# One prefill-and-stream step of a hybrid layer on one core: PSUM banks, linear-attention exponentials, output norm and the up-to-down seam rearranged

## The chip, the cores and the metric

The kernel runs on one core of a Trainium2 chip. A core has TensorE (PE, matrix products into the PSUM banks), VectorE (DVE), ScalarE (ACT), GpSimd (POOL) and SyncE (SP, which mostly issues transfers). The metric is the device time of one execution in microseconds (us): 1954.07, the median of three runs (1953.86 to 1955.78).

## The reference, cut to what matters

```python
h = rms_norm(x, g_pre_mix)
qa, ka, va, ra, alr, qb, kb, vb, ga, gb = split_cols(h @ w_in)
oa, s_gla = gla_branch(qa, ka, va, ra, alr, w_a2, b_a2, g_gla, gla_s0, gla_block)
ob, k_rows, v_rows = attn_fn(qb, kb, vb, rel_bias)
mix = (jax.nn.sigmoid(ga) * (oa @ w_br_a) + jax.nn.sigmoid(gb) * (ob @ w_br_b)) @ w_out
x = x + rms_norm(mix, g_post_mix)
f, conv_new = conv_ffn(rms_norm(x, g_pre_ffn), conv_s0, w_up, conv_w, conv_b, w_down)
x = x + rms_norm(f, g_post_ffn)
gate = jax.nn.sigmoid(rms_norm(x, g_pre_ple) @ w_ple_gate)
x = x + rms_norm(gate * (pe @ w_ple), g_post_ple)
...
# gla_branch, per head, b = cumulative log decay inside a block
decay = exp(where(j <= i, b[i] - b[j], -inf)); scores = sum_c q[i,c] k[j,c] decay[i,j,c]
o = scores @ v + (q * exp(b)) @ S;  S = exp(b_last) * S + (k * exp(b_last - b)).T @ v
o = rms_norm_per_head(o) * g_gla * silu(r)
```

There are 1024 prompt tokens and 32 sample tokens with the same weights, 1056 columns in all, D_MODEL 1024, four linear-attention heads (key 128, value 256), eight band-attention heads and a feed-forward width of 2816. All is fp32.

## The kernel before, in words

Activations lie with features on the 128 partitions and the 1056 tokens along the free dimension. An fp32 product is three matmuls on split operands: high times high, low times high, high times low (L230 to L232, L804 to L806, L1911 to L1913, L2356 to L2358). A split costs an ACT copy of the high half and a DVE subtraction for the low half. The wide layers (in, up, down) use one level of Strassen, so their products land in pairs of banks.

The eight PSUM banks are divided by `repsum` into three rotating sets: `mm` for the dense products, `one` for small ones, `two` for pairs. A matmul that wants the next bank of a set waits until that bank's last reader is done. In the band and linear-attention stages the division is `PS_BAND`: 3 `mm`, 3 `one`, 1 pair.

The stages that the change touches come in this order:

- *In-projection* (`in_strassen`, to 300 us): makes q, k, v and the gates; the gate rows silu(r) go to DRAM.
- *Band attention* (300 to 596 us) and *linear attention* (596 to 930 us). In both, units of a dense product (24 matmuls into one `mm` bank, L804 to L806, evacuated by ACT at L710 or L728 or by DVE at L786) fill the gaps of a chain of small steps; `piece()` issues a third of a unit, `flush()` evacuates what is complete.
- The linear attention goes through 16 segments u (4 heads of 4), 256 or 288 columns each. Tile `x` holds per segment the decay factors of seven levels: level l works on blocks of 2^l columns. `differences` (L1173, L1177, L1179, DVE) subtracts a reference column, `exponentials` (L1186, L1187, L1191, L1192, ACT) takes exp, `factors` (L1199, L1205, DVE) multiplies with q and k. `key_turns` (L1239) transposes level-7 rows on PE; `level_products` and `outputs` use the rest; `squares_a`, `sums_a`, `roots` and `results` are the per-head norm of the segment, spread over the neighbouring segments. `decays` (L1050 to L1072) prepares the log decays `b` of the next head. `branch_split` (L1415, L1416) splits the band result for its own projection, `branch_b`.
- *Output projection* (1100 to 1165 us): three chunks of 352 tokens, eight tiles each. Every tile is evacuated by a Copy (L1734); every second one is followed by a Square of the pair (L1607) and an addition on DVE. `norm_steps` is a generator that holds the two norms behind a chunk: `total` folds and splits the sum of squares, `inverse` adds it up over the partitions on PE (L1638, L1639) and takes the inverse root by Ln and Exp with one Newton step, `times` multiplies by norm weight and root (L1656), then the residual is added and the next norm's rows are split (ACT L1691, DVE L1685). `OUT_STEPS` and `UP_STEPS` say how many of its steps follow each tile of the next chunk or of the first up tiles. `log_exp` (L239) loads ACT's table for Ln and Exp.
- *Up* (to 1606 us), 22 tile pairs in Strassen form, with the convolution and gelu (`activate_steps`), results to DRAM as `d_b`; and *down*, which reads `d_b` back in rows (`row_load`), splits them (`row_split`: ACT L2050, DVE L2051) and its weights (`w_split`: ACT L2099, DVE L2100). The last up tile's closing additions (`ends`, L1953, L1954, `last_quarter` L1921 to L1923) stand among the first row splits.

PE, DVE and ACT run in the order in which the program is written. Transfers are issued from SP's and POOL's queues in a planner's order.

## Time and profile before

| | us |
|---|---|
| median of the runs | 1954.07 |
| profiled execution | 1952.56 |
| its span | 1950.6 |
| PE busy | 1898.7 |
| DVE busy | 1284.8 |
| ACT busy | 931.5 |
| POOL busy | 208.0 |

The granted clock of TensorE was 0.996 over the span. PE's busy time is the union of its matmuls, whose ends are modelled, so short waits between matmuls show better in the distance of two starts than in the idle column. In a row of waits stand the engine, the tile and line that waited, what ended the wait, the total, the number of times and the longest. In a row of a stretch stand its bounds and length, the busy time of PE, of its weight loads, of DVE, ACT and POOL, the granted clock, the DMA share and GB/s. In a row of a timeline stand start, duration, engine, line and tiles.

### The profile page before, as it was taken

How to read it: one execution, taken by the hardware profiler on the slowest of the kernel's cores; microseconds unless marked ns; L12 is line 12 of the kernel's file. 1: busy time of each engine (PE TensorE's matmuls, PEld its weight loads, DVE VectorE, ACT ScalarE, POOL GpSimd, SP SyncE). 2: the span in 40 equal slices, each digit the busy share in tenths (PEclk: the TensorE clock that was granted, in tenths of full speed). 3: DMA queues.
4: the chain of work that ended last, by engine and by line, in shares of the span. 5: the costliest groups of instructions: out<-in, count | busy, mean ns of one | idle time of the engine just before them, and what ended most of it. 6: DMA issues, size and time to landing. Idle time of an engine off the chain costs nothing.

```text
span 1950.6 us, 34919 instructions
## 1 busy us (share of the span) xinstructions
PE 1898.7 (97%) x13960; PEld 1861.5 (95%) x13960; DVE 1284.8 (66%) x2367; ACT 931.5 (48%) x1820; POOL 208.0 (11%) x352
## 2 busy tenths in 40 slices
PE   8999999999999999999999999999999999999996
PEld 8999999989999999999999999999999999999996
DVE  6855444555656776777544686877777766558776
...
GB/s 279 85 100 111 99 104 156 82 89 81 91 47 154 145 120 160 161 182 216 303 133 127 90 162 205 185 138 138 113 125 111 125 146 304 266 297 240 239 158 106
DMA packets 111119, 300.91 MB, mean 154 GB/s; under 512 B 12452, under 2 KB 34796, under 8 KB 110316
## 3 DMA queue, kind: packets, MB, share of 16 engines
...
q14 instruction: 54, 0.44, 0.1%
...
## 4 chain that ended last, share of the span: by engine, by line
PE 76%; DVE 12%; ACT 7%; issue 2%; DMA 2%; ACTq 0%; SPq 0%; DVEq 0%
PE two L1911 6%; PE two L1913 6%; PE two L1912 6%; PE mm L230 5%; PE mm L232 5%; PE mm L231 5%; PE mm L804 4%; PE mm L805 4%; PE mm L806 4%; PE two L2358 4%; PE two L2357 4%; PE two L618 4%; PE two L619 3%; PE two L2356 3%; PE two L620 3%
## 5 line engine op out<-in xcount | busy, mean ns | idle before, releaser
L804 PE MATMUL mm<-xh,whi 128*128 128x352 f32 x696 | 236.6, 340 | 0.0
L806 PE MATMUL mm<-xh,wlo 128*128 128x352 f32 x696 | 225.3, 324 | 0.0
L805 PE MATMUL mm<-xl,whi 128*128 128x352 f32 x696 | 224.6, 323 | 0.0
L2357 PE MATMUL two<-d,whi 128*128 128x264 f32 x616 | 174.8, 284 | 2.7 <-DVE d L2051 2.7
L2358 PE MATMUL two<-d,wlo 128*128 128x264 f32 x616 | 175.5, 285 | 1.2 <-DVE wlo L2100 1.2
L2356 PE MATMUL two<-d,whi 128*128 128x264 f32 x616 | 174.7, 284 | 0.1
L1913 PE MATMUL two<-mh,wlo 128*128 128x264 f32 x576 | 163.0, 284 | 0.0
L1912 PE MATMUL two<-ml,whi 128*128 128x264 f32 x576 | 162.9, 284 | 0.0
L1911 PE MATMUL two<-mh,whi 128*128 128x264 f32 x576 | 161.2, 284 | 0.0
L804 PEld LDWEIGHTS mm<-xh,whi 128*128 128x128 f32 x696 | 131.3, 189 | 1.7
L805 PEld LDWEIGHTS mm<-xl,whi 128*128 128x128 f32 x696 | 131.2, 189 | 0.4
L806 PEld LDWEIGHTS mm<-xh,wlo 128*128 128x128 f32 x696 | 130.5, 188 | 0.0
L2357 PEld LDWEIGHTS two<-d,whi 128*128 128x128 f32 x616 | 115.8, 188 | 3.3 <-DVE d L2051 3.3
L2358 PEld LDWEIGHTS two<-d,wlo 128*128 128x128 f32 x616 | 115.6, 188 | 1.7 <-DVE wlo L2100 1.7
L2356 PEld LDWEIGHTS two<-d,whi 128*128 128x128 f32 x616 | 116.4, 189 | 0.3 <-ACT d L2050 0.3
L1913 PEld LDWEIGHTS two<-mh,wlo 128*128 128x128 f32 x576 | 108.4, 188 | 0.0
L1912 PEld LDWEIGHTS two<-ml,whi 128*128 128x128 f32 x576 | 108.4, 188 | 0.0
L1911 PEld LDWEIGHTS two<-mh,whi 128*128 128x128 f32 x576 | 107.3, 188 | 0.0
L940 ACT ACTIVATE s<-s,sm 128x640 f32<-128x640 f32 (+5 forms) x72 | 50.6, 703 | 97.1 <-DVE sm L939 97.0
L1901 ACT ACTIVATE whi<-ws 128x512 fp32r<-128x512 f32 x72 | 45.2, 631 | 97.9 <-PE two L1912 72.7
L618 PE MATMUL two<-th,whi 128*128 128x264 f32 x320 | 90.8, 284 | 0.0
L619 PE MATMUL two<-tl,whi 128*128 128x264 f32 x320 | 90.8, 284 | 0.0
...
## 6 DMA issues: line engine op xcount, KB each, us to landing
...
```

Of the source, the lines that this page charges most:

```text
L230: pe.matmul(ps, h, xh(kt), start=(first and i == 0), stop=False)
L618: pe.matmul(ps[:, j, :HC], w[0][:, k], x[0](k, s), start=st, stop=False, skip_group_check=True)
L619: pe.matmul(ps[:, j, :HC], w[0][:, k], x[1](k, s), start=False, stop=False, skip_group_check=True)
L804: pe.matmul(ps, wh, h[:, k, s], start=(k == 0), stop=False)
L805: pe.matmul(ps, wh, l[:, k, s], start=False, stop=False)
L806: pe.matmul(ps, wl, h[:, k, s], start=False, stop=(k == cnt - 1))
L1911: pe.matmul(ps[:, j, :HC], w[0][:, k], x[0][:, k, s], start=st, stop=False, skip_group_check=True)
L1912: pe.matmul(ps[:, j, :HC], w[0][:, k], x[1][:, k, s], start=False, stop=False, skip_group_check=True)
L1913: pe.matmul(ps[:, j, :HC], w[1][:, k], x[0][:, k, s], start=False, stop=sp_, skip_group_check=True)
L2356: pe.matmul(o, wh, xh_[:, s], start=(k == 0 and p in (0, 4, 5)), stop=False, skip_group_check=True)
L2357: pe.matmul(o, wh, xl_[:, s], start=False, stop=False, skip_group_check=True)
L2358: pe.matmul(o, wl, xh_[:, s], start=False, stop=(k == HD - 1 and p in (3, 4, 6)), skip_group_check=True)
```

## The change

1. `PS_BAND` becomes 2 `mm`, 4 `one`, 1 pair. The loops that issue several units now flush after every piece.
2. Linear attention: levels 6 and 7 need no subtraction. ACT takes exp(b/16 minus a reference) directly, with the reference as a bias column from a small tile `refs` (25 columns per head, four small ACT copies); level 6 takes four operations of 64 columns, level 7 two of 128 (three with the sample columns) and one over the segment. The order becomes levels 1 to 4, 6, 7, and 5 last, and the factors of level 7 come first. The square of the inverse root goes from DVE to ACT, and the weight g_gla moves into the silu(r) rows (a Copy with a scale column per tile in `in_strassen`), so one multiplication replaces two.
3. The banks are divided anew before the second branch projection and not after it.
4. Output projection: every tile's Square is taken from its bank by ACT, beside a Copy with the norm weight as scale; the first norm then multiplies by the root alone (`g is None`). The table is loaded once, after the first chunk. A chunk's `total` is issued right behind its last tile, ahead of what is left of the norm of the chunk before, and the steps are spread differently. The first up tiles take both halves of chunk 0 before chunk 1.
5. Seam: in the last up tile the product s3 by t3 gets a pair of its own and comes before s1 by t1; its `ends` become a generator with three steps between the row splits; rows 2 and 3 of the first quarter are loaded early into a new pool `sx`.

```diff
@@ -50,7 +50,7 @@
 B_BUFS = 1
-PS_BAND = (3, 3, 1)
+PS_BAND = (2, 4, 1)
 BAND_GATES = (1, 1, 1, 0)
@@ -101,8 +101,8 @@
 RES_BUFS = 4
-OUT_STEPS = (1, 1, 2, 2, 2, 1, 1, 5)
-UP_STEPS = (1, 1, 2, 2, 2, 1, 1, 2, 3)
+OUT_STEPS = (1, 1, 1, 2, 2, 2, 2, 1)
+UP_STEPS = (0, 1, 2, 2, 2, 1, 2, 2, 2)
...
@@ -651,14 +651,18 @@
         ac.activation(z1, z1, f)
+        if gain is not None:
+            ac.activation(z1, z1, AF.Copy, scale=col(gain))
         dma.dma_start(d1, z1)
...
         ac.activation(z2, z2, f)
+        if gain is not None:
+            ac.activation(z2, z2, AF.Copy, scale=col(gain + 1))
         dma.dma_start(d2, z2)
...
     for n in range(0, 8, 2):
-        in_strassen(R0 + n, R0 + n + 1, AF.Silu, d_sr[n], d_sr[n + 1])
+        in_strassen(R0 + n, R0 + n + 1, AF.Silu, d_sr[n], d_sr[n + 1], G_GLA + n)
     for w0, d, top in ((GB0, d_gb, 8), (GA0, d_ga, GA_DENSE)):
@@ -1063,6 +1067,12 @@
         ac.activation(e[:, 8:9], b[:, T - 1 : T], AF.Exp, scale=-1.0 / TAU)
+        refs = g["refs"] = tl(gp, [P, 25], tag="refs", bufs=2)
+        ends = b[:, 0:NP].rearrange("p (n s) -> p n s", s=P)
+        ac.activation(refs[:, 0:8], ends[:, :, P - 1], AF.Copy, scale=-1.0 / TAU)
+        ac.activation(refs[:, 8:9], b[:, T - 1 : T], AF.Copy, scale=-1.0 / TAU)
+        ac.activation(refs[:, 9:17], ends[:, :, P // 2 - 1], AF.Copy, scale=-1.0 / TAU)
+        ac.activation(refs[:, 17:25], ends[:, :, P // 2 - 1], AF.Copy, scale=1.0 / TAU)
         yield
@@ -1166,25 +1176,25 @@
         x = X[u]
         for l in ls:
-            if l == 7:
-                break
             m, w = 1 << l, level_width(l, nt)
             bv = blocks(b[:, t0 : t0 + w], m)
             ve.tensor_tensor(blocks(x[:, l - 1, :w], m), bv, bv[:, :, m - 1 : m].to_broadcast([P, w // (2 * m), 2 * m]), op=ALU.subtract)
-        if ls[-1] < 7:
-            return
-        bv = b[:, t0 : t0 + 256].rearrange("p (n s) -> p n s", s=P)
-        ve.tensor_tensor(x[:, 6, :256].rearrange("p (n s) -> p n s", s=P), bv[:, :, P - 1 : P].to_broadcast([P, 2, P]), bv, op=ALU.subtract)
-        if nt > 256:
-            ve.tensor_tensor(x[:, 6, 256:nt], b[:, T - 1 : T].to_broadcast([P, NS]), b[:, NP:T], op=ALU.subtract)
...
     def exponentials(u, ls):
...
         for l in ls:
             if l == 7:
-                ac.activation(x[:, 6, :nt], x[:, 6, :nt], AF.Exp, scale=-1.0 / TAU)
+                for o in range(0, nt, P):
+                    n, w = (t0 + o) // P, min(P, nt - o)
+                    ac.activation(x[:, 6, o : o + w], g["b"][:, t0 + o : t0 + o + w], AF.Exp, scale=1.0 / TAU, bias=g["refs"][:, n : n + 1])
                 ac.activation(x[:, 7, :nt], g["b"][:, t0 : t0 + nt], AF.Exp, scale=-1.0 / TAU)
+                continue
+            if l == 6:
+                for o in range(0, 256, 64):
+                    up_, n = o // 64 % 2, (t0 + o) // P
+                    ac.activation(x[:, 5, o : o + 64], g["b"][:, t0 + o : t0 + o + 64], AF.Exp, scale=(-1.0 if up_ else 1.0) / TAU,
+                                  bias=g["refs"][:, 9 + 8 * up_ + n : 10 + 8 * up_ + n])
                 continue
             m, w = 1 << l, level_width(l, nt)
@@ -1344,6 +1354,7 @@
         ac.activation(y, y, AF.Exp, scale=-0.5)
+        ac.activation(r["sq"][:, 1, :n], y, AF.Square)
@@ -1351,11 +1362,9 @@
         y, ps, ot = r["z"], r["m"], r["ot"]
         t = r["sq"][:, 1, :nt]
-        ve.tensor_tensor(t, y, y, op=ALU.mult)
         ve.scalar_tensor_tensor(t, t, -0.5, ps, op0=ALU.mult, op1=ALU.mult)
         ve.scalar_tensor_tensor(t, t, 1.5, y, op0=ALU.add, op1=ALU.mult)
-        for j in range(2):
-            ve.scalar_tensor_tensor(ot[:, j, :nt], ot[:, j, :nt], col(G_GLA + 2 * h + j), t, op0=ALU.mult, op1=ALU.mult)
+        ve.tensor_tensor(ot[:, :, :nt], ot[:, :, :nt], t.unsqueeze(1).to_broadcast([P, 2, nt]), op=ALU.mult)
         ve.tensor_tensor(ot[:, :, :nt], ot[:, :, :nt], r["sr"][:, :, :nt], op=ALU.mult)
         dma.dma_start(d_oa[rows(h, t0, nt)].rearrange("j p t -> p j t"), ot[:, :, :nt])
@@ -1379,8 +1388,8 @@
     chain = steps
     next(chain)
-    differences(0, range(1, 8))
-    exponentials(0, range(1, 8))
+    differences(0, range(1, 6))
+    exponentials(0, (7, 6, 1, 2, 3, 4, 5))
     piece()
     piece()
@@ -1388,14 +1397,14 @@
         pass
-    factors(0, range(1, 8))
+    factors(0, (7, 1, 2, 3, 4, 5, 6))
     piece()
...
         piece()
-    flush()
+        flush()
@@ -1452,7 +1461,7 @@
         if u < 15:
-            exponentials(u + 1, range(1, 5))
+            exponentials(u + 1, (1, 2, 3, 4, 6, 7))
         if u == 15:
@@ -1460,9 +1469,9 @@
         flush()
         if u < 15:
-            differences(u + 1, range(5, 8))
-            factors(u + 1, range(1, 5))
-            exponentials(u + 1, range(5, 8))
+            differences(u + 1, (5,))
+            factors(u + 1, (7, 1, 2, 3, 4, 6))
+            exponentials(u + 1, (5,))
         steps_of(piece, 3)
         flush()
@@ -1470,7 +1479,9 @@
         if u < 15:
-            factors(u + 1, range(5, 8))
+            factors(u + 1, (5,))
+        else:
+            branch_split(2)
         if u >= 12:
@@ -1484,7 +1495,7 @@
                 piece()
-            flush()
+                flush()
             xp.release()
...
@@ -1511,6 +1520,7 @@
+    repsum((MODE, 8 - MODE, 0))
     gp.release()
@@ -1542,10 +1552,6 @@
     bo.release()
-
-    psum.release()
-    psum = tc.alloc_tile_pool(name="psum_wide", bufs=1, space=bass.MemoryType.PSUM, reuse_waits="tile")
-    banks[:] = [MODE, 8 - MODE, 0]
@@ -1637,7 +1643,6 @@
             pe.matmul(ps, ones["D"], l, start=False, stop=True)
-            log_exp()
             newton(out, ps, tmp)
@@ -1652,6 +1657,9 @@
         def times(i, g, r):
+            if g is None:
+                ve.tensor_tensor(zs[i], zs[i], r.unsqueeze(1).to_broadcast([P, 2, CW]), op=ALU.mult)
+                return
             for j in range(2):
                 ve.scalar_tensor_tensor(zs[i][:, j], zs[i][:, j], col(g + 2 * i + j), r, op0=ALU.mult, op1=ALU.mult)
@@ -1731,11 +1739,22 @@
             if c == NC - 1 and n in (4, 5):
                 up_weights(0, n - 4)
-            ac.activation(z[:, n], ps[:, :CW], AF.Copy)
-            if n % 2:
-                squares(zp, acc, n // 2, z[:, n - 1 : n + 1])
-        norm = norm_steps(zp, c, z, acc, G_POST_MIX, a["x"], d_x1, G_PRE_FFN,
+            if n % 2 == 0:
+                sq = acc if n == 0 else tl(zp, [P, 2, CW], tag="sq", bufs=2)
+            ac.activation(sq[:, n % 2], ps[:, :CW], AF.Square)
+            ac.activation(z[:, n], ps[:, :CW], AF.Copy, scale=col(G_POST_MIX + n))
+            if n == 3:
+                ve.scalar_tensor_tensor(acc, sq, 4 * EPS, acc, op0=ALU.add, op1=ALU.add)
+            elif n % 2 and n > 1:
+                ve.tensor_tensor(acc, acc, sq, op=ALU.add)
+        if c == 0:
+            log_exp()
+        rest = norm
+        norm = norm_steps(zp, c, z, acc, None, a["x"], d_x1, G_PRE_FFN,
                           lambda i, s=s: [t[:, 2 * i : 2 * i + 2, s] for t in (hh, hl)], d_hn)
+        next(norm)
+        for i in rest or ():
+            pass
     wo.release()
@@ -1804,7 +1823,8 @@
         bufs = {}
-        steps = [(f, j, c) for cs in ((0, 1), (2,)) for f in range(3) for j in range(2) for c in cs]
+        steps = [(0, 0, 0), (0, 1, 0), (0, 0, 1), (0, 1, 1)]
+        steps += [(f, j, c) for cs in ((0, 1), (2,)) for f in range(3) for j in range(2) for c in cs if f or c == 2]
...
@@ -1942,19 +1962,24 @@
             V, U = ps_pair(), ps_pair()
             V_, U_ = V[:, :, :HC], U[:, :, :HC]
+            W = ps_pair()
+            W_ = W[:, :, :HC]
             mul(V, weight(s2, WL_ENG[1]), "t2", True, True)
-            ve.tensor_tensor(q, p1, V_, op=ALU.add)
-            ve.tensor_tensor(c12, c12, q, op=ALU.add)
+            mul(W, weight(s3, WL_ENG[4]), "t3", True, True)
             mul(U, weight(s1, WL_ENG[2]), "t1", True, True)
-            ve.tensor_tensor(c12, c12, U_, op=ALU.add)
-            mul(V, weight(s3, WL_ENG[4]), "t3", False, True)
...
             def ends():
                 ve.tensor_tensor(q, p1, V_, op=ALU.add)
+                ve.tensor_tensor(c12, c12, q, op=ALU.add)
+                yield
+                ve.tensor_tensor(q, q, W_, op=ALU.add)
                 ve.tensor_tensor(c21, c21, q, op=ALU.add)
+                yield
+                ve.tensor_tensor(c12, c12, U_, op=ALU.add)
                 last_quarter(q, U)
-
-            return gx, av, ends
+                yield
+
+            return gx, av, ends()
         Y = ps_pair()
         Y_ = Y[:, :, :HC]
...
@@ -2006,6 +2034,8 @@
     order.__exit__(None, None, None)
     quarter_last()
+    sh.release()
+    sx = pool("sx")
     for f in (2, 3):
         activate(f, *open_[f, 0])
@@ -2039,7 +2069,7 @@
-            raws[p, i] = (sw_raw() if (p, i) < (0, 2) else tl(rp, [P, 2 * HT], tag="uraw", bufs=3)).rearrange("p (k t) -> p k t", k=2)[:, :n]
+            raws[p, i] = (sw_raw() if (p, i) < (0, 2) else tl(sx, [P, 2 * HT], tag=f"sraw{i}") if (p, i) < (0, 4) else tl(rp, [P, 2 * HT], tag="uraw", bufs=3)).rearrange("p (k t) -> p k t", k=2)[:, :n]
             dma.dma_start(raws[p, i], d_b[RSRC[p], 2 * i : 2 * i + n].rearrange("k p t -> p k t"))
@@ -2294,15 +2324,20 @@
     for i in range(1, 5):
         row_load(0, i)
-    for q in range(3):
+    for q in range(2):
         row_split(0, q)
         w_split(0, q)
+    next(last_up[2])
+    row_split(0, 2)
+    w_split(0, 2)
+    next(last_up[2])
     row_load(0, 5)
     row_split(0, 3)
+    next(last_up[2])
     row_load(1, 0)
-    last_up[2]()
     row_split(0, 4)
     row_load(1, 1)
+    sx.release()
     sw.release()
     last_rows_up = activate_steps(FT - 1, *last_up[:2])
```

On ACT in a linear-attention segment, before: the exponentials of a segment with the evacuation of a dense unit (`kq` from `mm`) between them, then the output of the segment before (`ot`).

```order
L1191 ACTIVATE x_7052<-x_7052 128x8x16
L1192 ACTIVATE x_7052<-x_7052 128x8x16
L728 ACTIVATE kq_6840<-mm_7066 128x352
L1191 ACTIVATE x_7052<-x_7052 128x4x32
L1192 ACTIVATE x_7052<-x_7052 128x4x32
L1191 ACTIVATE x_7052<-x_7052 128x2x64
L1192 ACTIVATE x_7052<-x_7052 128x2x64
L1186 ACTIVATE x_7052<-x_7052 128x256
L1187 ACTIVATE x_7052<-ev_6295 128x256
```

The same place after:

```order
L1201 ACTIVATE x_7066<-x_7066 128x8x16
L1202 ACTIVATE x_7066<-x_7066 128x8x16
L1196 ACTIVATE x_7066<-ev_6303,refs_6744 128x64 x4
L1190 ACTIVATE x_7066<-ev_6303,refs_6744 128x128 x2
L1191 ACTIVATE x_7066<-ev_6303 128x256
L732 ACTIVATE kq_6854<-mm_7080 128x352
L1201 ACTIVATE x_7066<-x_7066 128x4x32
L1202 ACTIVATE x_7066<-x_7066 128x4x32
```

Seven operations of levels 6 and 7 now stand ahead of the evacuation, and only the pair of level 5 behind it.

On DVE at the seam, before: the low halves of rows 2 and 3 (`d`) and of a weight, the closing additions of the last up tile, and row 4.

```order
L2051 TENSOR_TENSOR d_2466_17566<-uraw_17546,d_2466_17566 128x1056
L2100 TENSOR_TENSOR wlo_17570<-raw_17541,whi_17569 128x384
L2051 TENSOR_TENSOR d_2470_17575<-uraw_17548,d_2470_17575 128x1056
L1953 TENSOR_TENSOR c_2428_17307<-p_2427_17306,two_17435 128x528
L1954 TENSOR_TENSOR gx_17302<-gx_17302,c_2428_17307 128x528
L1921 TENSOR_TENSOR gx_17302<-c_2428_17307,two_17436 128x264
L1922 TENSOR_TENSOR gx_17302<-c_2428_17307,two_17436 128x232
L1923 TENSOR_TENSOR gx_17302<-c_2428_17307,two_17436 128x32
L2051 TENSOR_TENSOR d_2472_17585<-uraw_17550,d_2472_17585 128x1056
```

After, from the first closing addition to row 4:

```order
L1972 TENSOR_TENSOR c_2437_17341<-p_2436_17340,two_17469 128x528
L1973 TENSOR_TENSOR av_17337<-av_17337,c_2437_17341 128x528
L2081 TENSOR_TENSOR d_2476_17600<-sraw_2467_17578,d_2476_17600 128x1056
L2130 TENSOR_TENSOR wlo_17604<-raw_17573,whi_17603 128x384
L1975 TENSOR_TENSOR c_2437_17341<-c_2437_17341,two_17471 128x528
L1976 TENSOR_TENSOR gx_17336<-gx_17336,c_2437_17341 128x528
L2081 TENSOR_TENSOR d_2480_17611<-sraw_2468_17580,d_2480_17611 128x1056
L1978 TENSOR_TENSOR av_17337<-av_17337,two_17470 128x528
L1941 TENSOR_TENSOR gx_17336<-c_2437_17341,two_17470 128x264
L1942 TENSOR_TENSOR gx_17336<-c_2437_17341,two_17470 128x232
L1943 TENSOR_TENSOR gx_17336<-c_2437_17341,two_17470 128x32
L2081 TENSOR_TENSOR d_2482_17620<-uraw_17582,d_2482_17620 128x1056
```

The additions of the last up tile have moved between the rows, rows 2 and 3 come from tiles of their own, and row 4 is the first to use a `uraw` buffer.

21 lines of the change are left out of this document (11 added, 10 removed).

## The prediction

> **What bounds the kernel now.** I read the page's engine line first, then stretches of the program, then what TensorE (PE) waits for, then single rows at the waits.
>
> ```profile
> PE 1898.7 (97%) x13960; PEld 1861.5 (95%) x13960; DVE 1284.8 (66%) x2367; ACT 931.5 (48%) x1820; POOL 208.0 (11%) x352
> ```
> ```profile
> 300.00:600.00 300.00, 285.74 (x1951) 271.07 (x1950) 172.00 (x419) 180.41 (x445) 5.08 (x23) 1.00 0.32 91
> 600.00:900.00 300.00, 294.08 (x2004) 280.72 (x2003) 227.51 (x576) 147.64 (x435) 30.11 (x48) 1.00 0.58 160
> ...
> 1100.00:1200.00 100.00, 96.08 (x585) 93.90 (x584) 74.16 (x118) 52.42 (x89) 16.40 (x28) 1.00 0.47 154
> ...
> 1600.00:1650.00 50.00, 46.25 (x372) 45.20 (x371) 33.39 (x44) 24.78 (x36) 4.72 (x5) 1.00 0.93 300
> ```
>
> PE is busy 97% of the 1950.6 us span and the clock is full in all four stretches (column 1.00). The change leaves the number and form of the matmuls as they are, so it can only take PE's waits away or add some. PE's idle time is 1950.6 - 1898.7 = 51.9 us, and the four stretches the change touches hold 14.3 (band attention), 5.9 (gated linear attention), 3.9 (output projection) and 3.8 us (the seam from up to down). Who is waited for:
>
> ```profile
> PE two L933 <- DVE sm L939: 4.9, 8, 1.3
> PE one L987 <- DVE pt L949: 3.5, 9, 0.5
> PE one L911 <- DVE vs L908: 3.1, 3, 1.0
> PE two L2357 <- DVE d L2051: 2.7, 3, 1.6
> PE one L1239 <- DVE x L1199: 2.0, 1, 2.0
> PE one L1050 <- ACT b L1052: 1.8, 2, 1.1
> PE one L1638 <- ACT y L1632: 2.0, 2, 1.2
> PE mm L231 <- DVE ml L1685: 1.7, 3, 0.6
> PE two L2358 <- DVE wlo L2100: 1.2, 2, 1.0
> ```
>
> The idle column understates the loss, because a matmul's end is modelled. Starts say it better:
>
> ```profile
> 1146.76 0.33 PE L232 MATMUL mm<-mh,wlo 128*128 128x352 f32 x1
> 1146.92 0.32 PE L230 MATMUL mm<-mh,whi 128*128 128x352 f32 x1
> 1147.80 0.43 PE L231 MATMUL mm<-ml,whi 128*128 128x352 f32 x1 [0.56 <-DVE ml L1685]
> ```
>
> Such matmuls follow one another every 0.16 us (the first two); before the third 0.88 passed, so 0.72 is lost where the bracket says 0.56. Counting every gap in this way (start to start, less the usual step of the same form, gaps over 0.15 us; in the last two stretches over 0.09), I find 16.2 us lost in band attention, 13.4 in linear attention to 930 us, 5.9 in the output projection and 5.1 at the seam: 40.6 us, an upper bound on the gain.
>
> **Linear attention (16 segments).** Two causes carry the 13.4 us. The first is matmuls into the `one` banks whose last reader is late:
>
> ```profile
> 773.87 0.55 ACT L1052 ACTIVATE b<-one,nega 128x352 f32<-128x352 f32 x1
> ```
> ```profile
> 774.47 0.43 PE L1050 MATMUL one<-ev,wa 80*128 80x352 f32 x1 [1.14 <-ACT b L1052]
> ```
>
> L1052 reads one bank until 774.42 and L1050 starts 0.05 later in the same bank. Eight gaps of this kind sum to 5.1 us. The change gives `one` four banks instead of three, so each such matmul finds a bank one use older. I take 4.0, since the L1050s also come close to their data.
>
> The second is L1239 waiting for the level-7 rows (L1199): 2.17 at 599.5, then 0.25, 0.31, 0.31, 0.30, together 3.3 us. These rows come last now and first in the new order, and need no subtraction on VectorE (DVE), so I take all 3.3. Of the 3.1 us before the norm sums (L1338, L1339) I take 1.2, because the exponentials of two levels leave ScalarE's (ACT) queue ahead of L1324, and 0.5 of the 0.8 at 894.5, where DVE does less ahead.
>
> What it adds is ACT work ahead of an evacuation:
>
> ```profile
> L1191 ACT ACTIVATE x<-x 128x128 f32<-128x128 f32 x72 | 21.8, 303 | 86.2 <-DVE x L1173 86.2
> ...
> L710 ACT ACTIVATE ev<-mm 128x352 f32<-128x352 f32 x21 | 9.4, 445 | 3.5 <-PE mm L806 3.5
> ...
> L1051 ACT ACTIVATE ev<-one,vec 128x352 f32<-128x352 f32 x9 | 5.0, 556 | 0.0
> ...
> L1326 ACT ACTIVATE ot<-one 128x64 f32<-128x64 f32 x3 | 0.7, 224 | 2.0 <-DVE ss L1305 2.0
> ```
> ```profile
> L1354 DVE TENSOR_TENSOR sq<-sq 128x256 f32<-128x256 f32 x11 | 4.6, 418 | 5.9 <-ACT sq L1346 5.8
> ```
> ```profile
> 623.81 0.29 ACT L1191 ACTIVATE x<-x 128x128 f32<-128x128 f32 x1
> 624.01 0.29 ACT L1192 ACTIVATE x<-x 128x128 f32<-128x128 f32 x1
> 624.87 0.46 ACT L728 ACTIVATE kq<-mm 128x352 f32<-128x352 f32 x1 [0.56 <-PE mm L806]
> ```
>
> No row has an Exp with a bias column on 64 columns. Below it is L1326's 0.224 (no column operand); above it L1051's 0.556. A column operand costs 0.556 - 0.445 = 0.111 (L1051 against L710, same size), so I take 0.335 for 64 columns and 0.303 + 0.111 = 0.414 for 128. Neighbours start 0.10 before the last one ends (0.20 apart at 0.29 each), which gives a block of 4 x 0.235 + 2 x 0.31 + 0.30 = 1.9 us in front of the evacuation at 624.87; behind it four exponentials of about 1.0 us go. DVE starts the differences 0.4 us earlier (L1354 moves to ACT as a Square). The last pair ended at 624.30; the evacuation then starts near 624.3 + 1.9 - 0.4 = 625.8, 0.9 us later than now. What hides that:
>
> ```profile
> 625.48 0.41 PE L804 MATMUL mm<-xh,whi 128*128 128x352 f32 x1
> ...
> 631.18 0.41 PE L804 MATMUL mm<-xh,whi 128*128 128x352 f32 x1
> ```
>
> With two `mm` banks instead of three, the bank read until 626.3 is wanted at 631.18: almost 5 us of room. Where units follow faster (644 to 658 and after 914 us) the room by the same reading is 0.1 to 0.7 us, and I charge 1.0 there, plus 1.5 for late starts elsewhere in 16 segments (0 to 16 x 0.9 = 14). Sum: -4.0 - 3.3 - 1.2 - 0.5 + 2.5 = **-6.5 us** (-10 to +5). Folding g_gla into the gate rows costs 8 Copies of about 1.1 us on ACT before 150 us, where ACT is half idle and PE waits for nothing: 0.
>
> **Band attention.** L911 waits for a `one` bank that `vs` L908 still reads: 3.1 us in the list, 3.5 by starts. With a fourth bank it goes, but L987 behind it waits for data (`pt` L949), and L933 for the `two` bank (unchanged), so the PE then arrives earlier at the same DVE chain. I take 0.4 of each of three, and 0.3 for L987. Against it, at the start:
>
> ```profile
> 303.03 1.18 ACT L882 ACTIVATE kh<-ev 64x528 fp32r<-64x528 f32 x2 [6.79 <-DMA ev<-d_b]
> 304.11 0.44 ACT L710 ACTIVATE ev<-mm 128x352 f32<-128x352 f32 x1
> ```
>
> ACT waits there for a load, and the evacuation behind it ends at 304.55; the unit that would need that bank, with two, starts at 303.35. That is +1.2. Net 0 (-3 to +3).
>
> **Output projection.** Now a chunk's sums go to PE after two products of the next chunk, yet wait, since they stand behind the row work of the earlier chunk:
>
> ```profile
> 1113.19 0.89 DVE L1614 TENSOR_TENSOR accz<-accz,sq 128x704 f32<-128x704 f32 x1 [0.29 <-ACT sq L1607]
> ...
> 1115.21 0.53 DVE L1633 TENSOR_TENSOR y<-accz,y 128x352 fp32r<-128x352 f32 x1 [0.56 <-ACT y L1632]
> ```
> ```profile
> 1115.08 0.45 ACT L1734 ACTIVATE z<-mm 128x352 f32<-128x352 f32 x1
> 1115.55 1.28 ACT L239 ACT_TABLE_LOAD   x1
> ```
> ```profile
> L1656 DVE SCALAR_TENSOR_TENSOR z<-z,vec,rstd 128x352 f32<-128x352 f32 x24 | 12.7, 581 | 0.1
> ```
>
> After the change they follow one product, 24 matmuls at 0.163 = 3.9 us, and the row work of the earlier chunk comes behind them. The chain to be covered is, on ACT, Square and Copy of the last tile (two of 0.45, L1734's size) and at the first chunk the one table load that is left (1.28), beside them on DVE acc (0.89) and a fold at the size of L1633 (0.53); then y (0.45, L1734's size) and its low part (0.53). That is 2.2 + 1.0 = 3.2 us with the load and 2.9 without: it fits, with 0.7 us to spare. The rows of chunk 1 (`ml`, 1.7 us in the list, 2.6 by starts) are needed one unit of 3.9 us later, and DVE applies the first norm in one operation of 0.89 (L1614's size) for two of 0.58. Of the 5.9 I take **-4.5** (-5.9 to +1). Moving the division of the banks ahead of the second branch: no wait stands there in the trace, 0.
>
> [...] The rows show the load alone: 1.28 us, and 0.02 us from the end of L1734 to its start. [...]
>
> **Seam from up to down.**
>
> ```profile
> 1611.28 0.70 DVE L1953 TENSOR_TENSOR c<-p,two 128x528 f32<-128x528 f32 x1
> ...
> 1613.45 1.25 DVE L2051 TENSOR_TENSOR d<-uraw,d 128x1056 fp32r<-128x1056 f32 x1
> ```
> ```profile
> 1612.86 0.28 PE L2356 MATMUL two<-d,whi 128*128 128x264 f32 x1
> 1614.76 0.39 PE L2357 MATMUL two<-d,whi 128*128 128x264 f32 x1 [1.62 <-DVE d L2051]
> ```
>
> The low half of row 4 waits behind the four operations that end tile 21 (1611.28 to 1613.53), and row 3 (0.85 lost at 1611.4) behind its load. The change loads rows 2 and 3 many tiles ahead into room of their own, so the three `uraw` loads serve rows 4, 5 and 6, and splits the ends into steps between the rows. Running the new order with these durations, row 3 is done at 1608.7 (needed 1610.5), row 4 at 1611.5 (needed 1612.0), row 5 at 1612.8 (needed 1613.4). All but the 1.14 us at 1627.3 would go, half of which depends on the same DVE queue: **-4.0** (-5.1 to 0). On SP's queue the two early loads wait for stores of `d_b` that are long done.
>
> Sum: -6.5 + 0 - 4.5 - 4.0 = -15.0; I take -14.5, with half a microsecond for waits that the change has nothing to do with and that move. The profiled execution took 1952.56 us, 1.5 under the runs' median of 1954.07: 1952.56 - 14.5 + 1.5 = 1939.6.
>
> **Rivals.**
> - *Half of it comes back as the next wait.* PE arrives earlier at chains of ACT and DVE that did not get shorter, as in the band, where the wait after L911 is for data. Linear attention then gives -3, the output -2.5, the seam -2: -7.5, 1946.6. For it speaks DVE at 227.5 of 300 us in linear attention; against it, that the waits named have many microseconds of PE work between them.
> - *ACT becomes what linear attention waits for.* The 0.9 us of late evacuation shows on PE in each of 16 segments: +14 in place of the 2.5 charged, hence 1951. By ACT's 147.6 busy us of 300, plus some 20, it has room. [...]
> - *Two `mm` banks make it slower.* 696 L804 are 87 units of 8. If the product after next waits for its bank by 0.2 us each, that is 17 us, more than the gain; it decides above 14.5 / 87 = 0.17 us. With almost 5 us of room at 631 ACT would have to be late by that much throughout. Price at 0.25 each: 22, so 1962.
> - *The change does nothing*, if the waits named are for other things that share their semaphore: 1954.
>
> **How the numbers follow.** Forecast 0.62, half comes back 0.19, ACT 0.06, banks 0.07, nothing 0.04, more than forecast (to the full bounds, -10 - 2 - 5.9 - 5.1 = -23, 1931) 0.02. The range runs from 1931 to 1951, which takes in the first two rivals and leaves out about 0.15. Runs of this kernel tell no change from 0.2%, 3.9 us: faster is the forecast, its half and its upper bound, 0.83; same is ACT and nothing, 0.10; slower is the banks, 0.07.
>
> **What will show it.** Right: no wait of L1239 for L1199's rows and of L1050 for L1052; the two L1638 and three L231 waits gone; PE idle in 1600 to 1650 under 1 us. Wrong: L804 waiting for L710, L728 or L786 in 300 to 930 us; sums of the output waiting at their new place; row 4 of the seam still late because its load is.

## The result

The changed kernel takes 1942.44 us (median of 6 runs, 1941.27 to 1942.78). The kernel before, run beside it, takes 1953.96 us (6 runs, 1952.49 to 1957.41). The ratio is 0.9939, with a 95% interval of 0.9929 to 0.9949: 11.5 us faster, where 14.5 were forecast. The profiled execution took 1942.58 us, 10.0 less than that of before.

The engine line of the page after, and the five stretches of the program (columns: busy us of PE, PEld, DVE, ACT, POOL with their instruction counts, granted clock of PE, DMA share, GB/s):

```profile
PE 1896.0 (98%) x13960; PEld 1862.0 (96%) x13960; DVE 1258.7 (65%) x2287; ACT 959.0 (49%) x1919; POOL 210.2 (11%) x352
```
```profile
300.00:600.00 300.00, 286.48 (x1951) 271.68 (x1949) 168.61 (x409) 182.07 (x451) 4.69 (x22) 1.00 0.33 91
600.00:900.00 300.00, 297.65 (x2046) 286.04 (x2046) 213.52 (x528) 170.04 (x511) 31.48 (x50) 1.00 0.60 165
...
1100.00:1200.00 100.00, 100.00 (x621) 100.00 (x620) 73.76 (x109) 48.28 (x91) 17.06 (x30) 1.00 0.54 175
1250.00:1330.00 80.00, 78.33 (x641) 77.91 (x640) 60.86 (x99) 31.80 (x46) 10.86 (x28) 1.00 0.42 141
1600.00:1650.00 50.00, 48.74 (x395) 47.91 (x394) 31.85 (x45) 24.18 (x38) 6.18 (x7) 1.00 0.89 296
```

Linear attention gained, and the output projection no longer leaves PE idle at all. The fourth of these rows is new: PE is idle for 1.7 us between 1250 and 1330 us, in the first tiles of the up stage in Strassen form, where in the kernel before it was busy throughout:

```profile
1250.00:1330.00 80.00, 80.00 (x660) 80.00 (x659) 63.74 (x104) 31.97 (x46) 11.89 (x28) 1.00 0.42 138
```

Who is waited for in the changed kernel (columns: engine, tile and line that waits, engine, tile and line waited for, us in total, times, longest):

```profile
PE two L937 <- DVE sm L943: 7.5, 11, 1.2
PE one L991 <- DVE pt L953: 3.5, 9, 0.4
...
PE mm L808 <- ACT ev L714: 1.8, 2, 1.5
...
PE two L1931 <- DVE gx L1943: 1.5, 1, 1.5
PE mm L808 <- DVE ev L790: 1.4, 2, 0.8
...
PE two L2392 <- DVE d L2081: 0.8, 1, 0.8
PE mm L808 <- ACT kq L732: 0.8, 2, 0.5
```

(The line numbers have shifted by 4 to 35 against before: L933 is now L937, L939 is L943, L987 is L991, L911 is L915, L804 is L808, L1050 is L1054, L1151 is L1161, L1239 is L1249, L1338 is L1348, L2357 is L2392. Where a loss is named below, it is by the new numbers, unless the kernel before is meant.) The waits of L1050, L1239, L1638 and L231 have left the list. L808, the first product of a unit, which waits for the evacuation of its own bank, stands in it with six waits; in the kernel before it had one of 0.8 us (L804 for L786).

Counted as in the prediction (start to start, gaps over 0.15 us, over 0.09 in the output projection and at the seam; in linear attention less the 0.2 us steps between two forms of matmul, 2.3 us in every trace), PE loses:

| stage | before | after | difference | forecast |
|---|---|---|---|---|
| band attention, 300 to 596 us | 16.2 | 17.3 | +1.1 | 0 |
| linear attention, 596 to 930 us | 13.4 | 8.0 | -5.4 | -6.5 |
| output projection | 5.9 | 0 | -5.9 | -4.5 |
| up | 0 | 2.0 | +2.0 | 0 |
| seam from up to down | 5.1 | 2.3 | -2.8 | -4.0 |
| sum | 40.6 | 29.6 | -11.0 | -15.0 |

So the mechanisms stood where they were put, and what is missing lies in the up stage, where no wait had been looked for, at the head of the band, and in linear attention and at the seam, which gave about a microsecond less than forecast each. (The expectations below speak of 2.2 us in the up stage: that is with gaps from 0.09 us.) The five stages give 11.0 us where the profiled executions differ by 10.0: the changed kernel's is 0.7 us late at 100 us already, ahead of everything that the change touches. The experiments take these up.

### The profile page after: what moved, and what is told of

It is laid out like the page before. It is cut to its first block, busy times and chain, and to the rows that moved or that the text cites. A ratio compares the mean times of both kernels' runs of the same rounds, so it can differ in the third digit from the quotient of the medians.

```text
span 1940.9 us, 34940 instructions
## 1 busy us (share of the span) xinstructions
PE 1896.0 (98%) x13960; PEld 1862.0 (96%) x13960; DVE 1258.7 (65%) x2287; ACT 959.0 (49%) x1919; POOL 210.2 (11%) x352
## 4 chain that ended last, share of the span: by engine, by line
PE 75%; DVE 11%; ACT 7%; DMA 3%; issue 2%; ACTq 0%; SPq 0%; DVEq 0%
PE mm L230 6%; PE mm L232 6%; PE mm L231 6%; PE two L1931 6%; PE two L1932 6%; PE two L1933 6%; PE mm L808 4%; PE two L618 4%; PE two L619 4%; PE two L620 4%; PE mm L810 3%; PE mm L809 3%; PE two L2393 2%; PE two L2392 2%; PE two L2391 2%
## 5 line engine op out<-in xcount | busy, mean ns | idle before, releaser
L808 PE MATMUL mm<-xh,whi 128*128 128x352 f32 x696 | 236.8, 340 | 2.5 <-ACT ev L714 1.8
L2392 PE MATMUL two<-d,whi 128*128 128x264 f32 x616 | 174.7, 284 | 0.8 <-DVE d L2081 0.8
L1933 PE MATMUL two<-mh,wlo 128*128 128x264 f32 x576 | 163.3, 285 | 0.2 <-DVE wlo L1922 0.2
L1931 PE MATMUL two<-mh,whi 128*128 128x264 f32 x576 | 161.4, 285 | 1.5 <-DVE gx L1943 1.5
L808 PEld LDWEIGHTS mm<-xh,whi 128*128 128x128 f32 x696 | 131.3, 189 | 5.0 <-ACT ev L714 2.1
L2392 PEld LDWEIGHTS two<-d,whi 128*128 128x128 f32 x616 | 115.9, 188 | 1.2 <-DVE d L2081 1.2
L1931 PEld LDWEIGHTS two<-mh,whi 128*128 128x128 f32 x576 | 107.3, 188 | 1.7 <-DVE gx L1943 1.7
L1933 PEld LDWEIGHTS two<-mh,wlo 128*128 128x128 f32 x576 | 108.5, 188 | 0.4 <-DVE wlo L1922 0.4
L620 PE MATMUL two<-th,wlo 128*128 128x264 f32 x320 | 90.6, 284 | 0.0
```

What stands on the lines that cost most here:

```text
L620: pe.matmul(ps[:, j, :HC], w[1][:, k], x[0](k, s), start=False, stop=sp_, skip_group_check=True)
L808: pe.matmul(ps, wh, h[:, k, s], start=(k == 0), stop=False)
L1931: pe.matmul(ps[:, j, :HC], w[0][:, k], x[0][:, k, s], start=st, stop=False, skip_group_check=True)
L1933: pe.matmul(ps[:, j, :HC], w[1][:, k], x[0][:, k, s], start=False, stop=sp_, skip_group_check=True)
L2392: pe.matmul(o, wh, xl_[:, s], start=False, stop=False, skip_group_check=True)
```

## The experiments

All are edits of the changed kernel; each ran several times beside the kernel before. The runs of one kernel spread over 1.5 to 7.2 us, and most of the intervals below overlap that of the changed kernel (0.9929 to 0.9949). Clear of it are the late exponentials, the two combinations at the end and the banks 2, 2, 2; the own buffer touches it. So an experiment is read from its stage's loss, with the time beside it. All kernels issue 13960 matmuls, so the start of the nth can also be compared between two profiled executions, which shows where a difference in time arises ("matched" below).

| kernel | time, us | runs | ratio to before, 95% interval |
|---|---|---|---|
| banks 3, 3, 1 throughout | 1940.05 | 4 | 0.9934 (0.9920 to 0.9949) |
| banks split at linear attention | 1939.17 | 4 | 0.9929 (0.9914 to 0.9944) |
| no early loads | 1944.12 | 4 | 0.9956 (0.9941 to 0.9971) |
| output stage as before | 1944.99 | 5 | 0.9959 (0.9944 to 0.9973) |
| output arithmetic as before | 1938.84 | 4 | 0.9921 (0.9905 to 0.9938) |
| exponentials of levels 6, 7 late | 1950.27 | 10 | 0.9981 (0.9972 to 0.9990) |
| seam as before | 1945.35 | 4 | 0.9956 (0.9939 to 0.9973) |
| own buffer for the stored sum | 1937.98 | 4 | 0.9915 (0.9900 to 0.9929) |
| split banks and own buffer | 1935.96 | 4 | 0.9906 (0.9891 to 0.9920) |
| linear attention's norm as before | 1940.50 | 4 | 0.9929 (0.9915 to 0.9944) |
| three edits together | 1936.28 | 4 | 0.9907 (0.9892 to 0.9922) |
| the same with banks 2, 2, 2 in the band | 1976.50 | 4 | 1.0111 (1.0096 to 1.0126) |

### How the banks are divided

```diff
-PS_BAND = (2, 4, 1)
+PS_BAND = (3, 3, 1)
```

> The changed kernel with the old division of the banks (3 mm, 3 one, 1 pair) in band and linear attention; all else as changed. Theory: the fourth `one` bank and the lost third `mm` bank nearly cancel. Linear attention gets back its bank waits of L1249 and L1050 (4 to 5 us) and loses the waits of L808 for evacuations (0.47, 0.38, 0.63, 0.98, 0.76, 0.86 = 4.1 us); band attention wins about 1.1. So 1941 to 1943.5, against 1942.4 for the changed kernel. Rival, the banks carry the gain in linear attention: 1945 or more.

The three numbers are banks for `mm`, banks for `one`, and pairs for `two`. With three `mm` banks L808 no longer waits anywhere from 300 to 930 us (3.2 us in linear attention after the change, 1.7 at the head of the band). In exchange the bank waits of `one` are back: 2.65 us at L1054 and 1.87 at L1249. Linear attention loses 8.5 us, as against 8.0, and a wait for a load at its start is 0.8 of the 8.5 and 0.5 of the 8.0: the fourth `one` bank is worth the 4.0 us that the prediction gave it, and the missing `mm` bank takes them back (3.2 at L808 and a wait of 0.9 at L230). In the band L915 is at 3.5 us again and L937 at 6.2. The theory held for the waits; the time, 1940.05, is 1 us under its range. Matched, 1.0 us of that execution's lead arises ahead of the band and 1.0 at the seam, where the edit changes nothing.

```diff
+    repsum((2, 4, 1))
```

> The changed kernel with 3 mm, 3 one in band attention and 2 mm, 4 one from the first linear-attention segment on. Theory: the 1.67 us that L808 waits at 305.7 goes, while the 1.18 us waits of L915 return three times and the 0.97 us waits of L937 behind them go three times; band attention loses 16.2 us instead of 17.3, time 1941.3. Rival, the wait at 305.7 only hides a wait for data that comes next: no change, 1942.4.

This has 3, 3, 1 in the band and goes over to 2, 4, 1 ahead of the loop over the segments. Band 16.2, linear attention 6.6 us. L808 still loses 3.2 there: 0.44, 0.38, 0.62, 0.99 and 0.76. The time came out at 1939.17, below both expectations, but not all of that is the edit's. Matched with the changed kernel, 0.9 us of the lead arise ahead of the band and 0.9 at the seam, which the edit leaves alone; 1.1 are the band, as the theory has it, and 1.4 linear attention, of which 0.9 is a wait of L230 at 924 us for an `mm` bank, absent from all three traces with this division, and 0.5 a load. By the stages' losses this division is the better one; the runs don't tell it from 3, 3, 1 throughout (0.9914 to 0.9944 against 0.9920 to 0.9949).

The division is not free to go further. The last kernel of the table changes "three edits together" (below) to

```diff
-PS_BAND = (3, 3, 1)
+PS_BAND = (2, 2, 2)
```

> The same as e12_best with the banks 2, 2, 2 (mm, one, pairs) in band attention, so that a score product has a second pair of banks. Theory (L937 waits for the pair that DVE L943 still reads): L937 falls from 6.2 us to 2 or less, L915 with one bank less rises from 3.5 to 5 or 6; the band loses 12 to 14 us, 1932 to 1935. Rival (PE and DVE go in lockstep, so whatever bank is free, PE waits for DVE's chain): 16 to 20 us lost in the band, 1936 to 1940.

Neither was right. The waits list of this kernel:

```profile
PE one L908 <- DVE ev L958: 16.4, 7, 2.8
PE one L915 <- DVE pt L953: 9.0, 7, 1.6
PE one L950 <- DVE ev L958: 4.7, 8, 0.7
...
PE one L991 <- DVE pt L953: 1.6, 5, 0.3
```

The scores, L937, have left the list, which fits a wait for the pair rather than for DVE's chain (PE also comes later now, so it isn't proof). But with two banks of `one` the transposes (L908, L915, L950) wait for the readers of those banks, and the band loses some 41 us up to 596 us instead of 16.1. Of the 40 us by which the kernel is slower, these waits are about 25, matmuls at half clock in the band about 12 (last section), and linear attention the rest. I had priced the lost bank at about 2 us from one line of the list, L915; four lines use it.

### Linear attention: where the exponentials stand

```diff
-            exponentials(u + 1, (1, 2, 3, 4, 6, 7))
+            exponentials(u + 1, (1, 2, 3, 4))
...
-            factors(u + 1, (7, 1, 2, 3, 4, 6))
-            exponentials(u + 1, (5,))
+            factors(u + 1, (1, 2, 3, 4))
+            exponentials(u + 1, (5, 6, 7))
...
-            factors(u + 1, (5,))
+            factors(u + 1, (5, 6, 7))
```

> The changed kernel, with the exponentials of levels 6 and 7 by bias as now, but issued behind the evacuation, and their factors in the late group, as levels 5 to 7 were before. Theory: the new place of level 7 is what ended the waits of L1249 for its rows; 2.5 to 3.5 us of them come back, and of the 4.1 us in which L808 waits for an evacuation about half goes, since 1.9 us of ACT work no longer stands ahead of it: 1942.5 to 1944.5. Rival: the fourth bank of `one` alone ended those waits, so PE's loss from 596 to 930 us stays at 8 us or falls to 6: 1940.5 to 1942.4.

Neither theory had it. The stage loses 15.4 us, more than before the change, and the time goes back to 1950.27. Only 1.3 us of it is at L1249, where the theory put it. Most is at L1348 and L1349, the sums of the norm: 8.4 us against 2.0. ACT in one segment of this kernel (columns: start, us, engine, line, operation, tiles; in the bracket the idle time before, and what ended it):

```profile
688.77 1.05 ACT L1196 ACTIVATE x<-b,refs 128x64 f32<-128x64 f32 x4
689.73 0.68 ACT L1190 ACTIVATE x<-b,refs 128x128 f32<-128x128 f32 x2
690.31 0.40 ACT L1191 ACTIVATE x<-b 128x256 f32<-128x256 f32 x1
690.62 0.61 ACT L235 ACTIVATE whi<-raw 128x512 fp32r<-128x512 f32 x1
...
694.45 0.54 ACT L1056 ACTIVATE b<-one,nega 128x352 f32<-128x352 f32 x1
```
```profile
695.05 0.38 PE L1348 MATMUL one<-y,onesHr 128*128 128x256 f32 x1 [0.62 <-ACT b L1056]
```

The block of 1.9 us stands on ACT ahead of the evacuations and of `y`, and PE's norm sums come after all of them. In the changed kernel the block stands before the scores are copied, and PE has other products meanwhile. So the place of the two levels carries the gain of this stage. That the bias is what allows this place, because no subtraction on DVE has to come first, is argued; no run tests it.

The second question is whether that block holds up L808, as the rival with ACT had it. The evacuation at 626.55 in the changed kernel shows the cost as forecast:

```profile
624.69 1.06 ACT L1196 ACTIVATE x<-ev,refs 128x64 f32<-128x64 f32 x4
625.66 0.68 ACT L1190 ACTIVATE x<-ev,refs 128x128 f32<-128x128 f32 x2
626.25 0.40 ACT L1191 ACTIVATE x<-ev 128x256 f32<-128x256 f32 x1
626.55 0.44 ACT L732 ACTIVATE kq<-mm 128x352 f32<-128x352 f32 x1
```

The groups of this kernel's ACT instructions, with different shapes kept apart (busy us, mean ns):

```profile
L1196 ACT ACTIVATE x<-b,refs 128x64 f32<-128x64 f32 x48 | 12.7, 336 | 0.0
...
L1190 ACT ACTIVATE x<-b,refs 128x128 f32<-128x128 f32 x24 | 8.2, 390 | 0.0
```

An Exp with a bias column takes 0.336 us on 64 columns and 0.390 on 128, where 0.335 and 0.414 were estimated, and the block lasts the 1.9 us of the forecast. The evacuation behind it starts 0.7 us later than forecast (626.55 for 625.8), because the exponentials ahead of the block did not start earlier. With the block moved behind, one of L808's waits goes (0.47 at 645 us), another of 0.38 comes at 649.6, and the four others stay (0.38, 0.62, 0.99, 0.76). With three `mm` banks all five go. They are waits for a bank; ACT's block is behind one of them at most.

```diff
-        ac.activation(z1, z1, AF.Copy, scale=col(gain))
...
-        ac.activation(r["sq"][:, 1, :n], y, AF.Square)
...
+        ve.tensor_tensor(t, y, y, op=ALU.mult)
...
-        ve.tensor_tensor(ot[:, :, :nt], ot[:, :, :nt], t.unsqueeze(1).to_broadcast([P, 2, nt]), op=ALU.mult)
+        for j in range(2):
+            ve.scalar_tensor_tensor(ot[:, j, :nt], ot[:, j, :nt], col(G_GLA + 2 * h + j), t, op0=ALU.mult, op1=ALU.mult)
```

> The changed kernel, with the norm of linear attention as before (the square of 1/rms and the norm weight on VectorE, no weight in the gate rows). That is 0.42 + 2 x 0.58 - 0.89 = 0.7 us more VectorE work in each of 16 segments, and one ScalarE operation less. Theory (that work is on no path): 9.5 to 11 us lost from 596 to 930 us, as in the changed kernel (10.3), 1941.5 to 1943.5. Rival (VectorE is what linear attention waits for): 12 us or more, above 1944.5. Second rival (the Square on ScalarE stands ahead of evacuations): 9 us or less, under 1941.5.

(9.5 to 11 us in this expectation includes the 2.3 us of steps; so counted the run loses 9.3, without them 7.0.) That is 1.0 less than after the change, and the time, 1940.50, is the second rival's; but the difference is not the norm's. The kernel without early loads (below), whose linear attention is the changed kernel's to the letter, also loses 7.0: neither of the two waits for the load that costs the changed kernel's execution 0.5 at 598.8 us. Over the six such traces the stage loses 7.0 to 8.2. L1161 loses 0.5 less with the norm as before, L808 0.4 more. So the norm weight and the Square moved to ACT and the gate rows show no gain and no loss; of the change's parts for this stage, this is the one that could have been left out.

### Output projection: order or arithmetic

```diff
-OUT_STEPS = (1, 1, 1, 2, 2, 2, 2, 1)
-UP_STEPS = (0, 1, 2, 2, 2, 1, 2, 2, 2)
+OUT_STEPS = (1, 1, 2, 2, 2, 1, 1, 5)
+UP_STEPS = (1, 1, 2, 2, 2, 1, 1, 2, 3)
...
-        next(norm)
-        for i in rest or ():
-            pass
...
```

> The changed kernel with the output projection of before (Copy, Square of pairs from SBUF, table load for each root, old step tables, sums behind the older chunk's rows, old order of the first up tiles). Theory: the 5.9 us between 1100 and 1200 come back whole, 1948.3. Rival, part of them was made of PE arriving early and the gap closes elsewhere: 1945 or less.

With the whole stage of before, 5.7 us are lost in it again, so the theory has the stage right. In the up stage 1.9 us are lost at 1208 to 1211 us, for a weight's split, and nothing near 1307, which about cancels. The time, 1944.99, lies at the rival's bound and not at the theory's 1948.3 for another reason: matched with the changed kernel, this execution is 2.4 us ahead before the output stage begins and gains 1.0 at the seam, both in code that the edit leaves alone.

```diff
-            ac.activation(sq[:, n % 2], ps[:, :CW], AF.Square)
-            ac.activation(z[:, n], ps[:, :CW], AF.Copy, scale=col(G_POST_MIX + n))
+            ac.activation(z[:, n], ps[:, :CW], AF.Copy)
+            if n % 2:
+                squares(zp, acc, n // 2, z[:, n - 1 : n + 1])
...
-        norm = norm_steps(zp, c, z, acc, None, a["x"], d_x1, G_PRE_FFN,
+        norm = norm_steps(zp, c, z, acc, G_POST_MIX, a["x"], d_x1, G_PRE_FFN,
```

> The changed kernel, with the arithmetic of the output projection as before (Copy out of the bank, squares of a pair from SBUF, norm weight in DVE's row work) but the new order (sums ahead of the row work of the earlier chunk, one table load ahead). Theory: the order carries the gain of this stage. PE then loses at most 1.5 us between 1100 and 1200 us (5.9 before, 0 after), time 1941.5 to 1944. Rival: the arithmetic moved off DVE carries it: 3 us or more are lost there again, 1945 to 1948. The 2.2 us near 1307 us stay with both (in the run with the whole output stage of before they were gone).

Here only the order is new (with the single table load), and 0.34 us are lost where 5.9 were: the order carries all of it. Against the expectation the loss near 1307 us shrank to 0.6, and the time is 3.6 us below the changed kernel. Matched, the lead of this profiled execution arises at that place (1.5 us), at the head of the band, where a load came earlier (1.5), and at the seam (1.0). The last two don't belong to the edit.

### The loss near 1307 us

In the changed kernel PE stands at L1933 for 0.36 us at 1307.5, and at L1931 for 1.63 us at 1309.5. My first theory was that the two early loads of the seam collide with the store there:

```diff
-            raws[p, i] = (... tl(sx, [P, 2 * HT], tag=f"sraw{i}") if (p, i) < (0, 4) else tl(rp, ...
+            raws[p, i] = (... tl(rp, ...
```

> The changed kernel with rows 2 and 3 of the first quarter loaded late, as before the change (three uraw buffers); the steps of the last tile's closing additions stay. Theory: the 2.2 us that PE loses at 1307 to 1310 come from the early load of row 2, which takes DMA time from the store of gc that ACT waits for, so they go; at the seam the wait for the load of row 3 comes back, 0.9 to 3 us. Time 1941 to 1943, with 0 lost near 1307. Rival, the loss at 1307 comes from the order on DVE there and not from the load: 2.2 us stay, time 1943.3 to 1945.

The theory fell: 2.0 us are lost at the same place without them, and the time is in the rival's range. (The seam is read below.) In the changed kernel the trace shows on ACT:

```profile
1298.30 0.63 ACT L1921 ACTIVATE whi<-sraw 128x512 fp32r<-128x512 f32 x1 [1.78 <-issue]
1304.24 1.28 ACT L1782 ACTIVATE gc<-gx,vec 128x1058 f32<-128x1058 f32 x1 [5.31 <-DMA d_b<-gc]
1305.42 0.61 ACT L1921 ACTIVATE whi<-raw 128x512 fp32r<-128x512 f32 x1
1305.94 0.59 ACT L1992 ACTIVATE av<-two 128x528 f32<-128x528 f32 x1
```

`gc` has one buffer. Its head also holds the sum of two halves of a gated row, which is stored three times over into d_b. The next tile's first operation on `gc`, L1782, must wait for that store: 5.31 us, in which ACT has a weight's high half (L1921) and an evacuation queued behind it. The store was issued at 1297.65 on POOL's queue and took 6.5 us. In the kernel before ACT waited 2.30 us in the same way, which cost PE nothing:

```profile
1311.00 1.28 ACT L1763 ACTIVATE gc<-gx,vec 128x1058 f32<-128x1058 f32 x1 [2.30 <-DMA d_b<-gc]
```

There the store took 4.9 us, and ACT came to it 2.7 us after its issue, not 1.3. The test gives the sum its own buffer (2.1 kB a partition), so that `gc` is free when DVE has read it:

```diff
-        both, sm = av.rearrange("p (q t) -> p q t", q=2), gc[:, :HT]
+        both = av.rearrange("p (q t) -> p q t", q=2)
+        sm = gc[:, :HT] if f < 2 or f == FT - 1 else tl(sx, [P, HT], tag="sm", bufs=1)
```

> The changed kernel, with the sum of the two halves of a gated row (the three-fold store to d_b) in a buffer of its own from row 2 on, in place of the head of gc. ACT's first operation on gc then no longer waits for that store. Theory (the 2.2 us near 1307 us come from the store's 6.6 us, for which ACT stands with the weight's high half and the evacuation queued behind it): they go, 0.3 or less is left there, 1940.0 to 1940.8. Rival (DVE as a whole is behind PE there, because PE arrives earlier than before by what it no longer loses in the output projection): 1.5 us or more stay, 1941.8 to 1943.

ACT and the stretch in this kernel:

```profile
1297.26 0.63 ACT L1922 ACTIVATE whi<-sraw 128x512 fp32r<-128x512 f32 x1 [1.29 <-issue]
1300.16 0.63 ACT L1922 ACTIVATE whi<-raw 128x512 fp32r<-128x512 f32 x1 [2.27 <-PE two L1933]
1300.70 0.59 ACT L1993 ACTIVATE av<-two 128x528 f32<-128x528 f32 x1
...
1310.29 1.28 ACT L1782 ACTIVATE gc<-gx,vec 128x1058 f32<-128x1058 f32 x1 [0.29 <-DVE gx L2001]
```
```profile
1250.00:1330.00 80.00, 80.00 (x659) 80.00 (x658) 62.45 (x104) 31.54 (x46) 13.61 (x28) 1.00 0.46 158
```

PE is busy for all 80 us: the loss is gone, as in the three other kernels with the buffer. But the order has changed too. The text ahead says that PE, DVE and ACT run in the order in which the program is written; that holds only where the kernel fixes it (`order`, here up to L2035). In the up tiles from row 2 on a planner sets it, and with the sum in its own buffer it puts `gc` behind the evacuation `av`. So this run alone doesn't separate the buffer from the order. The traces do: ten kernels share `gc` for the sum and have the same order of ACT and DVE around it.

| kernel | ACT waits for the store, us | PE loses, us |
|---|---|---|
| before | 2.3 | 0 |
| output stage as before | 2.9 | 0 |
| output arithmetic as before | 3.9 | 0.6 |
| banks 3, 3, 1 throughout | 4.5 | 1.3 |
| seam as before | 5.3 | 2.0 |
| changed kernel | 5.3 | 2.0 |
| no early loads | 5.3 | 2.0 |
| linear attention's norm as before | 5.4 | 2.1 |
| banks split at linear attention | 5.5 | 2.2 |
| exponentials of levels 6, 7 late | 6.6 | 3.2 |

The first 3.3 us of the wait cost nothing, and each one beyond them costs PE one. That is the theory's answer, in one order of the instructions. The time fell by 4.5 us. Matched with the changed kernel, 2.2 of the lead arise at this place, 1.0 at the seam and 1.0 ahead of the band; the latter two don't belong to the edit.

### The seam

The kernel without early loads loses 4.8 us there. With the whole seam as before (the early loads out, as there, and the closing operations in one piece):

```diff
-            mul(V, weight(s2, WL_ENG[1]), "t2", True, True)
-            mul(W, weight(s3, WL_ENG[4]), "t3", True, True)
-            mul(U, weight(s1, WL_ENG[2]), "t1", True, True)
+            mul(V, weight(s2, WL_ENG[1]), "t2", True, True)
+            ve.tensor_tensor(q, p1, V_, op=ALU.add)
+            ve.tensor_tensor(c12, c12, q, op=ALU.add)
+            mul(U, weight(s1, WL_ENG[2]), "t1", True, True)
+            ve.tensor_tensor(c12, c12, U_, op=ALU.add)
+            mul(V, weight(s3, WL_ENG[4]), "t3", False, True)
...
-    next(last_up[2])
...
+    last_up[2]()
```

> The changed kernel, with the whole seam as before: no early loads of rows 2 and 3, and the four closing operations of the last up tile in one piece. Theory (the early loads carry the seam's gain, since without them alone 4.8 us were lost at the seam, against 2.3 in the changed kernel): 4.6 to 5.3 us lost from 1595 to 1650 us, 1943.5 to 1945.5. Rival (the closing operations in steps bring a gain of their own): 6 us or more, above 1946.

It loses 5.9 us, of which 2.4 are matmuls at half clock (0.22 us apart instead of 0.12) and 3.5 are waits. The loss is above the theory's 5.3 and the time inside its range. Counted over 0.15 us, so that the half-clock steps fall out, the kernel without early loads lost 4.4 and this one 3.5: without the early loads the closing operations in steps show no gain. The early loads are needed for the seam's gain; whether they bring it without the steps isn't shown, since no run has them alone. The 2.3 us of the changed kernel's profiled execution were 1.3 to 1.4 in each of the ten other traces with both edits: two waits of 0.4 for a weight's halves at 1632.5 and 1633.2 us are in that execution alone.

### A faster version

```diff
-PS_BAND = (2, 4, 1)
+PS_BAND = (3, 3, 1)
...
+    repsum((2, 4, 1))
...
+        sm = gc[:, :HT] if f < 2 or f == FT - 1 else tl(sx, [P, HT], tag="sm", bufs=1)
```

> Meant as the better version: banks 3, 3, 1 in band attention and 2, 4, 1 only from linear attention on, and the sum for d_b in its own buffer. If both gains add (1939.2 for the banks alone, 2.2 us for the buffer): 1936.5 to 1937.5. Rival: the buffer brings nothing, 1938.5 to 1940.

1935.96 us, 0.9906 of before (0.9891 to 0.9920): the gains add, and the 0.5 us under the expected range is less than the spread of the runs. It beats both kernels: its runs lie between 1934.65 and 1936.82, all under the lowest of the changed kernel. Of its lead over the changed kernel's profiled execution 1.1 us arise ahead of the band and 1.0 at the seam, which are not the edits'. With the output projection's arithmetic as before on top of it:

> Three edits that each helped, together: banks 3, 3, 1 in band attention, the sum for d_b in its own buffer, and the output projection's arithmetic as before in the new order. Band 16, linear attention 9, output 0.4, up 0, seam 1.1 us lost: 1935 to 1937. Rival: the output projection's DVE work comes back as a wait once the store's is gone, 1937.5 to 1939.

1936.28 us: no difference that can be told, and 0.34 us lost in the output stage, as in the kernel with that edit alone. The Copy with a norm weight and the Square from the bank are worth nothing measurable here.

## Why the prediction was right, and where it was off

**Sign and size.** 1939.6 was forecast, 1942.44 measured: faster, by four fifths of the forecast. The rival "half of it comes back as the next wait" (1946.6) is 4.2 us off and the forecast 2.8; part of that rival happened, in a stage in which it did not look. The closeness is in part luck. The sum was worked out on the profiled execution of before, which was 1.5 us under its median, and that of after is 0.14 us above its own. Between the two profiled executions the gain is 10.0 us, about two thirds of the 14.5; it is 11.5 between the medians. Of the prediction's own signs, the waits of L1050 and L1239 and those of the output projection went as it said, and two turned against it: the first product of a unit waits for L714, L732 and L790 (L710, L728 and L786 before), and PE is idle 1.26 us from 1600 to 1650 where under 1 was named (0.7 to 0.8 in the traces that lack the two waits at 1632.5 and 1633.2).

**Linear attention, -5.4 for -6.5.** The terms taken away were right: L1050 2.6 to 0 and L1239 5.3 to 0.2, together 7.7 for the 4.0 + 3.3 forecast; L1338 and L1339 3.1 to 2.0 for the 1.2. The term added was too small: 2.5 us were charged, less 0.5 for L805 (2.0), and L808, L230, L1227 and L1161 lose 5.6 us where L804, L805 and L1151 lost 2.3, which is 3.3 more. Its cause was put down to ACT's block; the runs put four of L808's five waits down to the two banks.

**Band, +1.1 for 0.** L915 fell from 3.5 to 0.5 and L937 rose from 6.2 to 9.3 behind it, which the prediction foresaw as PE arriving earlier at the same chain; so the gain it took (1.2 for L915 and 0.3 for L987) was not there. The +1.2 at the head came as 1.67:

```profile
304.11 1.18 ACT L886 ACTIVATE kh<-ev 64x528 fp32r<-64x528 f32 x2 [7.20 <-DMA ev<-d_b]
305.19 0.44 ACT L714 ACTIVATE ev<-mm 128x352 f32<-128x352 f32 x1
```
```profile
305.69 0.43 PE L808 MATMUL mm<-xh,whi 128*128 128x352 f32 x1 [1.51 <-ACT ev L714]
```

It hangs on when a load arrives: over the eight traces with banks 2, 4, 1 in the band it was between 0 and 1.9 us. Their loss in the band is 15.3 to 17.2 us, 16.4 on average, against 16.0 to 16.1 in the five with 3, 3, 1; so the net 0 of the forecast was right, and most of the +1.1 is this one execution. The rival that two banks of `mm` cost 0.25 us at every unit did not happen; L808 lost 1.7 + 3.2 = 4.9 us to them from the band's head to 930 us.

**Output, -5.9 for -4.5.** The room of 0.7 us was enough, and the reserve of 1.4 was not needed. The price was split between order and arithmetic nowhere in the prediction; it is all the order, the single table load included.

**Seam, -2.8 for -4.0,** or -3.8 by the ten other traces. Right, but of the two edits only the early loads are shown to matter.

**The step that failed** is that nothing would be lost elsewhere, beyond half a microsecond: the prediction left the up stage out of its sum, and 2.0 us are lost there. It asked which waits go, and not what PE arrives at earlier after 1200 us. The row that could have told it was in the trace of before: ACT at 1311.00 waiting 2.30 us for a store of the very buffer that it is to write, with an evacuation behind it. That was a wait on the edge of the path: it could grow by 1.0 us, to 3.3, before PE lost anything, and it grew by 3.0. Half of that is the store, 6.5 us for 4.9, and why it took longer is not shown; the other half is ACT's earlier arrival.
